# A first tile normalised after its projection, and a last tile in pieces of 384 and 128 columns

## The chip, the cores and the metric

The kernel runs on one core of one Trainium2 chip, as one program on five engines: TensorE (PE in the profile; its weight loads have a row of their own, PEld), VectorE (DVE), ScalarE (ACT), GpSimd (POOL) and SyncE (SP), which issues most of the transfers. The metric is the device time of one execution in microseconds (us), the lower the better.

## The reference, cut to what matters

Two request groups, 256 and 512 tokens of 1024 values each, go through the same two layers. Each layer has a token mixer (windowed attention in the first, differential attention in the second) and a dense channel mixer. Each of these four sub-layers stands between two norms:

```python
def rms_norm(x, g):
    y = x * lax.rsqrt(jnp.mean(x * x, axis=-1, keepdims=True) + RMS_EPS)
    return y * g

def swiglu(h, w_gate_up, w_down):
    g, u = jnp.split(h @ w_gate_up, 2, axis=-1)
    return (jax.nn.silu(g) * u) @ w_down

for i in range(DEPTH):                                   # DEPTH = 2
    h = rms_norm(x, norm_mix_pre[i])
    m = window_gqa_sink(h, ...) if i % 2 == 0 else diff_attention(h, ...)
    x = x + rms_norm(m, norm_mix_post[i])
    h = rms_norm(x, norm_ffn_pre[i])
    x = x + rms_norm(swiglu(h, ffn_w_gate_up[i], ffn_w_down[i]), norm_ffn_post[i])
```

The first thing that the first mixer does is one product, `qkv = h @ w_in`. A row of `x` divided by its root mean square is the row times one number, so that number may be applied before this product or after it.

## The kernel before, in words

The 768 tokens are six tiles of 128 rows, numbered 0 to 5. Every float32 product is made of three products of a rounded type (called fp32r in the rows): an operand is cut into a high part (`hi`, a cast on ACT) and the rest (`lo`, a subtraction on DVE), and hi by hi, hi by lo and lo by hi are added up in PSUM. These are lines 315, 316 and 317, with a new 128 by 128 weight load before each. The weights stream from DRAM and are cut the same way (lines 222 and 223).

At the start, `load_x`, `gain` and `fetch` queue on SP the loads of tile 0's x, of the first norm's gains (broadcast over the partitions into `gpre`), of two weight pieces, of tile 1's x and of two more weight pieces. For a tile, `enter` makes the normed rows: line 365 squares x and sums on ACT, line 359 adds epsilon on ACT, line 360 takes the power -1/2 on POOL, line 369 multiplies x by this number and by the gains on DVE. `entered` (and, for tile 0, the code below it) transposes the rows on PE (line 407), cuts them into hi and lo (lines 303 and 304), and enters the tile after the next. Two copies of an identity matrix in other types (lines 85 and 87) are made on DVE as well; the first transposes do not use them.

In `mixer_a`, `unit(i)` is the product of one tile with one of four groups of 384 columns (64 columns times four query heads, one key head and one value head). Its `end` reads the product from PSUM: the values (line 589, ACT) and the rotary positions (lines 530 to 536, DVE).

At the end, `ffn(1)` has seven products per tile over the columns of `w_down` (a product of 2 by 2 blocks in seven multiplications). In the last of them, tiles 3 and 4 each get 512 columns in one bank, and tile 5 gets its 512 columns in two pieces of 256 with a bank each (`last_product`), so that the first piece can be finished on DVE and ACT while PE makes the second. For each piece `k`, DVE adds what was there before (line 1169), ACT squares and sums (line 1291), and DVE multiplies by the gains (line 1293), in place. Then ACT and POOL make the norm's number (lines 359 and 360), and `last_tile` multiplies by it, adds x and stores, in two halves (lines 495 and 497). `begin(t)` loads the x that is added; its place is one of two buffers, and tile 5's buffer is the one from which tile 3's result is stored.

The order of the instructions on each engine is fixed when the program is built: a scheduler places them by priority and by its own estimate of when each is ready. Each engine then runs its own list strictly in that order and waits on semaphores.

Of the kernel before, what the change touches and what calls it, by code (L numbers as in the profile page):

```python
# [9 lines left out]
F32 = mybir.dt.float32  # L10
F32R = mybir.dt.float32r
BF16 = mybir.dt.bfloat16
AF = mybir.ActivationFunctionType
ALU = mybir.AluOpType
# [3 lines left out]
P = 128  # L18
D = 1024
KT = D // P  # L20
HD = 64
# [11 lines left out]
HALF = 384  # L33
# [13 lines left out]
def trunk(  # L47
# [19 lines left out]
    nc = tc.nc  # L67
    const = ctx.enter_context(tc.tile_pool(name="const", bufs=1))
# [3 lines left out]
    gpool = ctx.enter_context(tc.tile_pool(name="gpool", bufs=1))  # L72
# [5 lines left out]
    def bank(name):  # L78
        return ps.tile([P, 512], F32, tag="ps", name=name)
# [26 lines left out]
    nsink = const.tile([P, 16], F32, name="nsink")  # L106
    subl = const.tile([P, 1], F32, name="subl")
    nlam = const.tile([P, 1], F32, name="nlam")

    def small_inputs():  # L110
        nc.sync.dma_start(out=cos_sb, in_=cos)
# [79 lines left out]
    def load(dst, src):  # L191

        with ExitStack() as after:
            if dpool[0] is not None:
                after.enter_context(tc.issue_after(state["load"].ins))
            state["load"] = nc.sync.dma_start(out=dst, in_=src)
# [166 lines left out]
    def row_rstd(src, junk, name):  # L363
        ss = small.tile([P, 1], F32, tag="ss", name=f"ss_{name}")
        nc.scalar.activation(out=junk, in_=src, func=AF.Square, scale=D ** -0.5, accum_out=ss)
        return rstd(ss, eps_sb[:, 0:1], name)

    def scaled(y, src, r, g):
        state["scaled"] = nc.vector.scalar_tensor_tensor(out=y, in0=src, scalar=r, in1=g, op0=ALU.mult, op1=ALU.mult)

    def new_y(name):
        return scr.tile([P, D], F32, tag="y", name=f"y_{name}")
# [16 lines left out]
    x_at = [x_in]  # L389
# [134 lines left out]
    def rope(ap, dst, src, n, t, name):  # L524

        pos = t - seq_of(t)[0]
        t1 = ap.tile([P, n, HD], F32, tag="rope1", name=f"r1_{name}", bufs=1)
        t2 = ap.tile([P, n, HD], F32, tag="rope2", name=f"r2_{name}", bufs=1)
        h = HD // 2
        nc.vector.tensor_tensor(  # L530
            out=t1[:, :n], in0=src, in1=cos_sb[:, pos:pos + 1, :].broadcast_to([P, n, HD]), op=ALU.mult)
        nc.vector.tensor_tensor(
            out=t2[:, :n, :h], in0=src[:, :, h:], in1=sin_sb[:, pos:pos + 1, :h].broadcast_to([P, n, h]), op=ALU.mult)
        nc.vector.tensor_tensor(
            out=t2[:, :n, h:], in0=src[:, :, :h], in1=sin_sb[:, pos:pos + 1, h:].broadcast_to([P, n, h]), op=ALU.mult)
        nc.vector.tensor_tensor(out=dst, in0=t1[:, :n], in1=t2[:, :n], op=ALU.add)
# [30 lines left out]
    def mixer_a(gp, g_next, first_steps, o):  # L567
        with ExitStack() as st:
# [4 lines left out]
            def unit(i):  # L573

                gi, t = divmod(i, NT)
                first, n = seq_of(t)
                if t == 0:
                    wk[gi] = column_blocks(take(4), HALF)
                elif t in (2, 4):
                    free(6 - t // 2)  # L580
                pm = bank(f"pqa_{i}")
                steps = product_steps(pm[:, :HALF], [(htile(t, k), wk[gi][k]) for k in range(KT)])
                if t == NT - 1:
                    steps = releasing(steps, 4, 2)

                def end():
                    if t == first:
                        vv[gi, first] = ap.tile([P, n, HD], F32, tag=f"v{first}", name=f"va{gi}_{first}", bufs=2)
                    nc.scalar.copy(out=vv[gi, first][:, t - first], in_=pm[:, 320:384])
                    qk = ap.tile([P, 5, HD], F32, tag="qk", name=f"qk{i}", bufs=2)  # L590
                    rope(ap, qk, pm[:, :320].rearrange("p (n d) -> p n d", d=HD), 5, t, f"a{i}")

                    sp = ap.tile([P, 6, 2, HD], F32R, tag="sp", name=f"sp{i}", bufs=2)
                    nc.scalar.copy(out=sp[:, 0:4, 0], in_=qk[:, 0:4])
                    nc.scalar.copy(out=sp[:, 4], in_=qk[:, 4:5].broadcast_to([P, 2, HD]))
                    nc.vector.tensor_tensor(
                        out=sp[:, 0:4, 1], in0=qk[:, 0:4], in1=sp.bitcast(F32)[:, 0:4, 0], op=ALU.subtract)
                    nc.vector.tensor_tensor(
                        out=sp[:, 5], in0=qk[:, 4:5].broadcast_to([P, 2, HD]), in1=sp.bitcast(F32)[:, 4], op=ALU.subtract)

                    def turn():
                        if t == first:
                            kh[gi, first] = ap.tile([P, n * P], F32R, tag=f"kh{first}", name=f"kha{gi}_{first}")
                            kl[gi, first] = ap.tile([P, n * P], F32R, tag=f"kl{first}", name=f"kla{gi}_{first}")
                        q[i] = ap.tile([P, 4, P], F32R, tag="q", name=f"qa{i}", bufs=4)
                        tq, tk = ps.tile([P, 512], F32R, tag="ps", name=f"tqa{i}"), ps.tile([P, 512], F32R, tag="ps", name=f"tka{i}")
                        at = slice((t - first) * P, (t - first + 1) * P)
                        for j in range(2):
                            nc.tensor.transpose(tk[:, j * P:(j + 1) * P], sp[:, 4 + j].rearrange("p a d -> p (a d)"), ident_r)
                        for j in range(4):  # L610
                            nc.tensor.transpose(tq[:, j * P:(j + 1) * P], sp[:, j].rearrange("p a d -> p (a d)"), ident_r)
                        nc.scalar.copy(out=kh[gi, first][:, at], in_=tk.bitcast(F32)[:, 0:P])
                        nc.scalar.copy(out=kl[gi, first][:, at], in_=tk.bitcast(F32)[:, P:2 * P])
                        nc.scalar.copy(out=q[i].rearrange("p h n -> p (h n)"), in_=tq.bitcast(F32))

                    pending[i] = turn

                return steps + [end]
# [321 lines left out]
    def ffn(layer, later, comb, cpool, cstack, ostack, gains):  # L940
# [182 lines left out]
        with ExitStack() as st:  # L1123
# [7 lines left out]
            def run(p, gs, wk, tiles, into, first=None, last=None, w=512, part=0, more=True):  # L1131

                gs = list(gs)
                todo = [(g, j) for g in gs for j in range(min(2, NPAIR - 2 * g))]
                for n, (g, j) in enumerate(todo):
                    a = acts.of(p, g)
                    b = tuple(v[:, j * 512 + part:j * 512 + part + w] for v in wk[g])
                    for i in tiles:
                        products(
                            into[i][:, :w], [(tuple(v[:, j, i * P:(i + 1) * P] for v in a), b)],  # L1140
                            first and n == 0, bool(last) and n == len(todo) - 1, more and p > 2)
# [16 lines left out]
            def begin(t):  # L1158
                x_of[t] = xpool.tile([P, D], F32, tag="x", name=f"x{sub}_{t}")
                load(x_of[t], x_at[sub][t])  # L1160
# [7 lines left out]
            def add(t, c, b):  # L1168
                nc.vector.tensor_tensor(out=y[t][:, c], in0=b, in1=y[t][:, c], op=ALU.add)
# [56 lines left out]
            free(2)  # L1226

            V2 = [bank(f"pv2_{k}") for k in range(2)] if final else []

            def last_product(i, gs, wk, first=False, last=False, parts=(0, 1)):  # L1230

                if final and i == 2:
                    for k in parts:
                        run(6, gs, wk, [i], {i: V2[k]}, first, last, 256, 256 * k, False)
                else:
                    run(6, gs, wk, [i], V, False, last)

# [14 lines left out]
            free(0)  # L1252
            stage(2, 3)
            begin(4)
            gs = range(3, NGRP)
            wk = dict(zip(gs, take(3)))
            for g in gs:
# [26 lines left out]
            for k in range(2):  # L1284
                last_product(2, gs, wk, last=True, parts=(k,))
                if k == 0:
                    stage(4, 1)
                    begin(5)
                c = slice(256 * k, 256 * k + 256)
                add(5, c, V2[k][:, :256])  # L1290
                nc.scalar.activation(
                    out=junk[:, c], in_=y[5][:, c], func=AF.Square, scale=D ** -0.5, accum_out=ss4[:, k:k + 1])
                nc.vector.tensor_tensor(out=y[5][:, c], in0=y[5][:, c], in1=gp[:, c], op=ALU.mult)
                if k == 0:
                    nc.scalar.activation(out=ss[:, 0:1], in_=ss4[:, 0:1], func=AF.Identity, bias=ss[:, 0:1])
# [67 lines left out]
    y_in = {}  # L1363

    def enter(t):
        x = xs_sb[t]
        y_in[t] = new_y(f"pre0_{t}")
        scaled(y_in[t], x, row_rstd(x, y_in[t], f"pre0_{t}"), g_in)

    def entered(t):  # L1370
# [108 lines left out]
```

## Time and profile before

| what | value |
|---|---|
| time, median of 3 runs | 1687.2 us (1686.35 to 1689.65) |
| the profiled execution's own time | 1688.34 us |
| its span, first to last instruction | 1686.6 us |
| PE busy | 1659.1 us, 98% of the span |
| DVE, ACT, POOL busy | 1251.3, 949.7 and 81.7 us (74%, 56%, 5%) |
| mean granted TensorE clock | 0.997 |

PE is busy nearly everywhere, so the table says that a microsecond can be gained only where PE waits or where PE has nothing left to do. Rows of the timeline tell where that is: a row starts with its start and its duration in us, and a bracket at its end gives how long the engine had been idle before it and what ended the wait. A matmul's row is longer than the time between two of them, since they are pipelined; the time between the starts of neighbours is its pace.

### The profile page before, as it was taken

Reading aid. Unit: us, or ns where it says so; the run is one execution under the profiler, and the core shown is the slowest. Engines: PE = TensorE matmul, PEld = TensorE weight load, DVE = VectorE, ACT = ScalarE, POOL = GpSimd, SP = SyncE. Lnnn points to the kernel's source line nnn. Section 1 sums busy time; section 2 is a strip of 40 time slices with the busy share of each in tenths; the row PEclk is TensorE's granted clock in tenths of the full one; section 3 lists DMA queues with packets and bytes.
Section 4 is the critical chain, followed back from the end, with each engine's and each line's share of the span. In section 5 each row is a group of like instructions: output and inputs, shape, how many; then the busy total and the mean of one; then the engine's idle time right before and its main releaser. Section 6 shows DMA issues by size and latency. Waiting matters only on the chain. (4 is left out here: it accounts for less than half of the span.)

```text
span 1686.6 us, 25513 instructions
## 1 busy us (share of the span) xinstructions
PE 1659.1 (98%) x9483; PEld 1514.3 (90%) x9483; DVE 1251.3 (74%) x2488; ACT 949.7 (56%) x2158; POOL 81.7 (5%) x104
## 2 busy tenths in 40 slices
PE   7999999999999999999999999999899999999998
PEld 7888878899999998888999999988799999998887
DVE  7888766896766666988777676874997666666886
ACT  6777775654444444556566666674744444444553
POOL 1000001000000000001000000331000000000001
PEclk9999999999999999999999999999999999999999
DMA  6111014534333347666211111113444343336765
GB/s 212 39 38 48 14 38 150 175 134 140 109 125 99 128 139 250 230 235 205 83 39 38 38 38 38 48 51 113 170 138 141 108 141 108 128 114 226 249 222 176
DMA packets 62107, 207.30 MB, mean 123 GB/s; under 512 B 6752, under 2 KB 8928, under 8 KB 61728
## 3 DMA queue, kind: packets, MB, share of 16 engines
q1 hardware_dynamic: 55152, 175.15, 30.8%
q0 software_dynamic: 6688, 30.28, 5.6%
q8 instruction: 74, 1.21, 0.3%
q14 instruction: 49, 0.40, 0.1%
q10 hardware_dynamic: 144, 0.26, 0.0%
HBM read 162.80 MB, written 42.86 MB: 122 GB/s over the span
## 5 line engine op out<-in xcount | busy, mean ns | idle before, releaser
L223 DVE TENSOR_TENSOR wlo<-wraw,whi 128x1024 fp32r<-128x1024 f32 (+2 forms) x180 | 204.9, 1144 | 173.9 <-ACT whi L222 172.7
L222 ACT CAST whi<-wraw 128x1024 fp32r<-128x1024 f32 (+2 forms) x180 | 176.5, 986 | 117.4 <-PE py L316 58.9
L315 PE MATMUL py<-hhi,whi 128*128 128x384 f32 x464 | 155.4, 335 | 0.8 <-ACT u L976 0.8
L317 PE MATMUL py<-hhi,wlo 128*128 128x384 f32 x464 | 155.0, 334 | 0.0
L316 PE MATMUL py<-hlo,whi 128*128 128x384 f32 x464 | 155.0, 334 | 0.0
L315 PE MATMUL pqb<-whi,hhi 128*128 128x384 f32 x384 | 136.5, 356 | 0.0
L316 PE MATMUL pqb<-wlo,hhi 128*128 128x384 f32 x384 | 128.9, 336 | 0.0
L317 PE MATMUL pqb<-whi,hlo 128*128 128x384 f32 x384 | 128.8, 335 | 0.0
L303 ACT CAST hhi<-araw 128x768 fp32r<-128x768 f32 (+1 forms) x74 | 57.6, 783 | 94.6 <-DMA araw<-act 94.2
L317 PE MATMUL pv<-whi,hlo 128*128 128x512 f32 (+1 forms) x240 | 92.2, 384 | 0.4 <-DVE hlo L304 0.4
L315 PE MATMUL pv<-whi,hhi 128*128 128x512 f32 (+1 forms) x240 | 92.4, 385 | 0.0
L316 PE MATMUL pv<-wlo,hhi 128*128 128x512 f32 (+1 forms) x240 | 92.1, 384 | 0.0
L304 DVE TENSOR_TENSOR hlo<-araw,hhi 128x768 fp32r<-128x768 f32 (+1 forms) x74 | 65.2, 889 | 32.3 <-ACT hhi L303 32.1
L315 PEld LDWEIGHTS py<-hhi,whi 128*128 128x128 f32 x464 | 87.1, 188 | 1.7 <-ACT u L976 1.4
L316 PEld LDWEIGHTS py<-hlo,whi 128*128 128x128 f32 x464 | 87.1, 188 | 0.0
L317 PEld LDWEIGHTS py<-hhi,wlo 128*128 128x128 f32 x464 | 87.1, 188 | 0.0
L315 PE MATMUL po<-whi,hhi 128*128 128x512 f32 x192 | 77.9, 406 | 0.2 <-ACT hhi L303 0.2
L317 PE MATMUL po<-whi,hlo 128*128 128x512 f32 x192 | 75.4, 393 | 0.2 <-DVE hlo L304 0.2
L316 PE MATMUL po<-wlo,hhi 128*128 128x512 f32 x192 | 75.3, 392 | 0.0
L315 PEld LDWEIGHTS pqb<-whi,hhi 128*128 128x128 f32 x384 | 72.3, 188 | 2.0 <-issue 1.7
L315 PE MATMUL pqa<-whi,hhi 128*128 128x384 f32 x192 | 73.9, 385 | 0.0
L315 PE MATMUL px<-hhi,whi 128*128 128x384 f32 x208 | 70.8, 342 | 2.7 <-ACT hhi L303 2.7
(303 smaller groups left out, 4829.6 us busy)
## 6 DMA issues: line engine op xcount, KB each, us to landing
act<-st POOLq DMA_DIRECT2D x22, 1344.0 KB, 6.6
wraw<-in_wgu SPq DMA_DIRECT2D x56, 512.0 KB, 4.6
araw<-act SPq DMA_DIRECT2D x70, 384.0 KB, 4.0
y_wraw<-in_wgu SPq DMA_DIRECT2D x40, 512.0 KB, 3.6
wraw<-in_wd SPq DMA_DIRECT2D x40, 512.0 KB, 3.9
wraw<-in_wb SPq DMA_DIRECT2D x32, 384.0 KB, 3.2
xd<-x SPq DMA_DIRECT2D x18, 512.0 KB, 3.0
x<-xd SPq DMA_DIRECT2D x18, 512.0 KB, 4.1
```

Of the source, the lines that this page charges most:

```text
L222: state["raw_hi"] = nc.scalar.copy(out=hi, in_=src)
L223: state["raw_lo"] = nc.vector.tensor_tensor(out=lo, in0=src, in1=hi.bitcast(F32), op=ALU.subtract)
L303: state["hi"] = nc.scalar.copy(out=hi, in_=src)
L304: state["lo"] = nc.vector.tensor_tensor(out=lo, in0=src, in1=hi.bitcast(F32), op=ALU.subtract)
L315: nc.tensor.matmul(out, ah, bh, start=start and i == 0, stop=False, skip_group_check=more)
L316: nc.tensor.matmul(out, ah, bl, start=False, stop=False, skip_group_check=more)
L317: nc.tensor.matmul(out, al, bh, start=False, stop=stop and i == last, skip_group_check=more)
```

## The change

There are three parts, and one of the places is in two functions.

First, tile 0's rows are no longer multiplied by the norm's number before they are transposed: `enter(0)` multiplies x by the gains alone, and the number goes into a small tile `r0` (a copy on POOL). The squares go to a scratch buffer of their own. In `mixer_a`, the four products of tile 0 are read from PSUM once, by an ACT instruction that multiplies by `r0` and writes a tile `pm0` in SBUF; the values and the rotary positions then read this tile.

Second, in the last `ffn`, tile 5's x is loaded right behind tile 4's, into the place of `gpre`, which the last sub-layer doesn't use.

Third, tile 5's two pieces have 384 and 128 columns in place of 256 and 256.

```diff
 def end():
+    src = pm
+    if t == 0:
+        src = ap.tile([P, HALF], F32, tag="pm0", name=f"pm0_{gi}")
+        nc.scalar.activation(out=src, in_=pm[:, :HALF], func=AF.Copy, scale=r0)
     if t == first:
         vv[gi, first] = ap.tile([P, n, HD], F32, tag=f"v{first}", name=f"va{gi}_{first}", bufs=2)
-    nc.scalar.copy(out=vv[gi, first][:, t - first], in_=pm[:, 320:384])
+    nc.scalar.copy(out=vv[gi, first][:, t - first], in_=src[:, 320:384])
     qk = ap.tile([P, 5, HD], F32, tag="qk", name=f"qk{i}", bufs=2)
-    rope(ap, qk, pm[:, :320].rearrange("p (n d) -> p n d", d=HD), 5, t, f"a{i}")
+    rope(ap, qk, src[:, :320].rearrange("p (n d) -> p n d", d=HD), 5, t, f"a{i}")
...
 V2 = [bank(f"pv2_{k}") for k in range(2)] if final else []
+cols = [slice(0, 384), slice(384, 512)]
...
-            run(6, gs, wk, [i], {i: V2[k]}, first, last, 256, 256 * k, False)
+            run(6, gs, wk, [i], {i: V2[k]}, first, last, cols[k].stop - cols[k].start, cols[k].start, False)
...
 begin(4)
+if final:
+    x_of[5] = gpool.tile([P, D], F32, tag="gpre", name=f"x{sub}_5")
+    load(x_of[5], x_at[sub][5])
...
     if k == 0:
         stage(4, 1)
-        begin(5)
-    c = slice(256 * k, 256 * k + 256)
-    add(5, c, V2[k][:, :256])
+    c = cols[k]
+    add(5, c, V2[k][:, :c.stop - c.start])
...
 def enter(t):
     x = xs_sb[t]
     y_in[t] = new_y(f"pre0_{t}")
+    if t == 0:
+        state["scaled"] = nc.vector.tensor_tensor(out=y_in[t], in0=x, in1=g_in, op=ALU.mult)
+        nc.gpsimd.tensor_copy(out=r0, in_=row_rstd(x, new_y("sq0"), "pre0_0"))
+        return
     scaled(y_in[t], x, row_rstd(x, y_in[t], f"pre0_{t}"), g_in)
```

The scheduler also moves instructions. On DVE at the start of the program, these are the rows before (`y_pre` is the tile's rows before the transposes, `tp_h` the transposed rows in PSUM, `wlo` and `hlo` the lo parts of weights and rows, `ident_r` and `ident_b` the two copies of the identity):

```order
L85 CAST ident_r<-ident 128x128
L87 CAST ident_b<-ident 128x128
L369 SCALAR_TENSOR_TENSOR y_pre_0_162<-x_0_138,rstd_pre_0_165,gpre_140 128x1024
L223 TENSOR_TENSOR wlo_170<-wraw_142,whi_169 128x768
L223 TENSOR_TENSOR wlo_176<-wraw_144,whi_175 128x768
L304 TENSOR_TENSOR hlo_113<-tp_h_0_0_181,hhi_111 128x4x128
L304 TENSOR_TENSOR hlo_113<-tp_h_0_1_188,hhi_111 128x4x128
```

and now:

```order
L1378 TENSOR_TENSOR y_pre_0_163<-x_0_139,gpre_141 128x1024
L224 TENSOR_TENSOR wlo_173<-wraw_143,whi_172 128x768
L85 CAST ident_r<-ident 128x128
L87 CAST ident_b<-ident 128x128
L224 TENSOR_TENSOR wlo_179<-wraw_145,whi_178 128x768
L305 TENSOR_TENSOR hlo_114<-tp_h_0_0_184,hhi_112 128x4x128
L305 TENSOR_TENSOR hlo_114<-tp_h_0_1_191,hhi_112 128x4x128
```

The first multiplication has lost an operand, and the two casts of the identity stand between the two `wlo`. The list of ACT is the same there: the two weight casts stand ahead of tile 0's `hhi`.

On DVE at the end of the program (`yf` is the sub-layer's result, `pv` a bank, `x` the tile that is added and stored), before:

```order
L1154 TENSOR_TENSOR yf_4_16415<-pv_1_16600,gpost_16144 128x512
L472 SCALAR_TENSOR_TENSOR x_4_17567<-yf_4_16415,rstd_post_4_17610,x_4_17567 128x1024
L1169 TENSOR_TENSOR yf_5_16416<-pv_0_17474,yf_5_16416 128x256
L1169 TENSOR_TENSOR yf_5_16416<-pv_1_17475,yf_5_16416 128x256
L1293 TENSOR_TENSOR yf_5_16416<-yf_5_16416,gpost_16144 128x256 x2
L495 SCALAR_TENSOR_TENSOR x_5_17632<-yf_5_16416,rstd_last,x_5_17632 128x512 x2
```

and now:

```order
L1159 TENSOR_TENSOR yf_4_16426<-pv_1_16611,gpost_16155 128x512
L473 SCALAR_TENSOR_TENSOR x_4_17578<-yf_4_16426,rstd_post_4_17623,x_4_17578 128x1024
L1174 TENSOR_TENSOR yf_5_16427<-pv_0_17485,yf_5_16427 128x384
L1301 TENSOR_TENSOR yf_5_16427<-yf_5_16427,gpost_16155 128x384
L1174 TENSOR_TENSOR yf_5_16427<-pv_1_17486,yf_5_16427 128x128
L1301 TENSOR_TENSOR yf_5_16427<-yf_5_16427,gpost_16155 128x128
L496 SCALAR_TENSOR_TENSOR x_5_17580<-yf_5_16427,rstd_last,x_5_17580 128x512 x2
```

The first piece's multiplication by the gains, which writes in place and waits until ACT has squared the piece, now stands ahead of the second piece's addition. On SP, tile 5's load moves from behind tile 3's store to ahead of it; nothing else moves there at the end.

## Rows read from the trace of the kernel before

**Rows 1.** Waits of PE, whole span: in total, times, longest (us)

```profile
PE tp_h L407 <- DVE y_pre L369: 8.1, 1, 8.1
```

**Rows 2.** Tile `gpre`, 0 to 20 us: issue (duration ns, start) and landing

```profile
L376 SPq DMA_DIRECT2D gpre<-in_g_pre x1: 421/421/421, 1.2 to 1.2; - x1
...
DMA to landing us min/median/max: 5.4/5.4/5.4
```

**Rows 3.** Timeline of all engines, first 12 us

```profile
1.45 0.45 DVE L85 CAST ident_r<-ident 128x128 fp32r<-128x128 f32 x1 [0.52 <-POOL ident masks.py:199]
...
1.67 0.30 DVE L87 CAST ident_b<-ident 128x128 bf16<-128x128 f32 x1
...
5.82 0.55 POOL L360 TENSOR_TENSOR rstd_pre<-rstd_pre,mhalf 128x1 f32<-128x1 f32 x1 [4.00 <-ACT rstd_pre L359]
...
6.76 1.28 DVE L369 SCALAR_TENSOR_TENSOR y_pre<-x,rstd_pre,gpre 128x1024 f32<-128x1024 f32 x1 [4.79 <-POOL mask_r L93]
...
8.52 2.02 DVE L223 TENSOR_TENSOR wlo<-wraw,whi 128x768 fp32r<-128x768 f32 x2 [0.48 <-ACT whi L222]
8.71 0.83 ACT L222 CAST whi<-wraw 128x768 fp32r<-128x768 f32 x1 [0.23 <-DMA wraw<-in_wa]
...
9.45 1.24 ACT L303 CAST hhi<-tp_h 128x512 fp32r<-128x512 f32 x2
...
11.19 0.69 PE L317 MATMUL pqa<-whi,hlo 128*128 128x384 f32 x1
```

**Rows 4.** The same timeline, two later weight loads of PE

```profile
18.10 0.86 PEld L407 LDWEIGHTS tp_h<-ident,y_pre 128*128 128x128 f32 x8 [0.42 <-DVE y_pre L369]
...
23.58 0.19 PEld L317 LDWEIGHTS pqa<-whi,hlo 128*128 128x128 f32 x1 [0.51 <-DVE hlo L304]
```

**Rows 5.** Timeline of all engines, from 1675 us

```profile
1675.65 0.28 PE L315 MATMUL pv<-whi,ahi 128*128 128x256 f32 x1
...
1675.85 0.60 ACT L1153 ACTIVATE y_pd<-pv 128x512 f32<-128x512 f32 x1 [2.32 <-PE pv L317]
...
1676.57 0.69 DVE L1154 TENSOR_TENSOR yf<-pv,gpost 128x512 f32<-128x512 f32 x1 [1.10 <-ACT y_pd L1153]
...
1677.59 1.28 DVE L472 SCALAR_TENSOR_TENSOR x<-yf,rstd_post,x 128x1024 f32<-128x1024 f32 x1 [0.33 <-POOL rstd_post L360]
...
1678.79 0.42 DVE L1169 TENSOR_TENSOR yf<-pv,yf 128x256 f32<-128x256 f32 x1
...
1679.12 0.28 PE L317 MATMUL pv<-whi,alo 128*128 128x256 f32 x1
1679.24 0.42 ACT L1291 ACTIVATE y_last<-yf 128x256 f32<-128x256 f32 x1 [2.31 <-DVE yf L1169]
...
1679.98 0.40 ACT L1291 ACTIVATE y_last<-yf 128x256 f32<-128x256 f32 x1
...
1680.94 0.55 POOL L360 TENSOR_TENSOR rstd_last<-rstd_last,mhalf 128x1 f32<-128x1 f32 x1 [3.38 <-ACT rstd_last L359]
1682.15 1.42 DVE L495 SCALAR_TENSOR_TENSOR x<-yf,rstd_last,x 128x512 f32<-128x512 f32 x2 [1.21 <-DMA x<-xd]
```

**Rows 6.** Timeline of PE, 899 to 906 us, in the second mixer

```profile
899.97 0.33 PE L315 MATMUL pqb<-whi,hhi 128*128 128x384 f32 x1
...
901.88 0.34 PE L317 MATMUL pqb<-whi,hlo 128*128 128x384 f32 x1
...
902.27 1.06 PE L871 MATMUL pob<-vb,aT 128*128 128x128 f32 x8
903.09 0.42 PE L315 MATMUL pqb<-whi,hhi 128*128 128x384 f32 x1
```

**Rows 7.** Timeline of PE, 25.2 to 26.4 us: transposes of fp32r

```profile
25.93 0.51 PE L611 MATMUL tqa<-ident_r,sp 128*128 128x128 f32 x4
26.28 0.41 PE L315 MATMUL pqa<-whi,hhi 128*128 128x384 f32 x1
```

**Rows 8.** Groups of weight loads by form: busy us, mean ns, idle before

```profile
L315 PEld LDWEIGHTS pv<-whi,ahi 128*128 128x128 f32 x35 | 6.6, 189 | 1.0
```

More of the change, by code (lines that the diff above doesn't have):

```diff
@@ L108, in trunk @@
     nlam = const.tile([P, 1], F32, name="nlam")
+    r0 = const.tile([P, 1], F32, name="r0")
     def small_inputs():
```

## Prediction

> **What bounds the kernel now.** I read the page first: PE is busy 98% of the span, so a change can pay only where PE waits or after its last product. The view of waits says where PE waits: one wait of 8.1 us, at the start, for tile 0's normed rows [rows 1]; no other single wait comes near it. So there are two places, and the timeline is read there: the first 25 us, where the order in which DMA, ACT and DVE get ready decides, and the last 11 us, from tile 5's first piece at 1675.65 to the last multiplication at 1682.15 and the store behind it [rows 5]. In between, every product and every weight load stays as it is.
>
> **Start: the norm's number.** It leaves the path, but was it last? The power on POOL ends at 5.82 + 0.55 = 6.37. The gains, which the same DVE instruction reads, were issued at 1.2 and landed 5.4 later, at 6.6 [rows 2], and the instruction began at 6.76 [rows 3]. The bracket there names POOL because POOL's next instruction ended late; the transfer is the later one. The new multiplication needs the gains as well, so it begins at 6.7 or so and saves at most 0.1.
>
> Nor would an earlier end help. ACT casts the second weight piece from 8.71 to 9.54 (it waits for that transfer), and tile 0's `hhi` stands behind it and begins at 9.45 [rows 3]. ACT's list is the same now. The first product therefore starts when it did.
>
> **Start: the moved casts.** In DVE's new list the two identity casts stand behind the first `wlo`. Before, they ran from 1.45 to 1.97, 0.52 together, in idle time. The two `wlo` ran back to back from 8.52 to 10.54, and `hlo` followed; the first product that needs `hlo` started at 11.19 [rows 3]. Now the first `wlo` ends at 8.52 + 1.01 = 9.53, when the second piece's cast is just done (9.54), so the casts push the second `wlo` and both `hlo` by about 0.45 to 0.5, and the product at 11.19 goes to about 11.65. I take +0.45.
>
> Some of this comes back. Before, PE's weight loads waited twice more, 0.42 us for tile 2's rows and 0.51 us for tile 2's `hlo` [rows 4]. A load runs one product ahead, so each costs the products that less one pace of 0.17: 0.25 and 0.34. In the new lists tile 1's first `hlo` stands ahead of tile 2's multiplication, tile 2's transposes stand seven products later, and tile 2's first `hlo` stands ahead of tile 3's multiplication. Both waits should go: -0.59. Together with the 0.1 the start is worth 0.45 - 0.59 - 0.1, about -0.2. Bounds: -0.7 (the casts find a gap) to +0.5 (both waits stay).
>
> The four reads of tile 0's product cost ACT some 0.5 us each (a 384-column read, by the widths below), in a stage in which PE is the bound; POOL's copy is beside the path. I take 0.
>
> **End: tile 5's x.** Before, the last multiplication began at 1682.15, after a wait of 1.21 for x. The norm's number was there at 1680.94 + 0.55 = 1681.49 [rows 5]. With x loaded early, what is late next is that number: a gain of 1682.15 - 1681.52 = 0.63, if nothing else moves. The load itself goes out behind tile 4's, more than ten us ahead, and no queue waits for it.
>
> **End: the pieces.** Each of tile 5's eleven blocks takes three products per piece, so 33 pairs of products (18 before the last five blocks, 15 in them). A 256-column product has a pace of (1679.12 - 1675.65)/29 = 0.1197 [rows 5], a 384-column one of (901.88 - 899.97)/11 = 0.1736 [rows 6]. A pair was 0.2394 and is 0.1736 + c, where c is the pace of a 128-column fp32r product with its own weight load. The trace has none, so c is bounded:
> - The line through 384 and 256 gives 0.1197 - 0.0539 = 0.066, the lower end: the pair costs the same as before.
> - Four 128-column fp32r transposes, each with its own load, took 26.28 - 25.93 = 0.35, or 0.087 each [rows 7].
> - Eight records of the plain float32 product of 128 columns took 903.09 - 902.27 = 0.82 [rows 6]; the program has two records for each such product, so 0.205, the upper end.
>
> I take c = 0.12. The weight load does not get shorter with the columns (0.189 in this stage, for pieces of 512 and 256 columns [rows 8]), and a 256-column product is the narrowest fp32r product that the trace shows behind such a load.
>
> The Trainium skill (TensorE: Matmul & The Clock Gate, section "LDWEIGHTS (loading the stationary operand)") says that a load takes the number of columns over 1.2 ns, so 107 ns for 128, whatever the product's width. That rule speaks against this change: c could not fall under 0.107, and the sum by it would be +0.8 at the end in place of +1.1. The load's row of 0.189 is longer than the rule's figure, but rows overlap, so the row does not refute it.
>
> Now the chain. PE's 18 early pairs push all that follows by 18 x (0.1736 + 0.12 - 0.2394) = 0.97, tiles 3 and 4 too. Tile 4's multiplication goes from 1677.59 to 1678.56 and ends at 1679.84. Widths: DVE took 0.69 for 512 and 0.42 for 256 columns, so 0.56 for 384 and 0.29 for 128; ACT 0.60 and 0.42, so 0.51 and 0.30 [rows 5]. The first piece's addition runs 1679.76 to 1680.32, its square to 1680.86 and its sum is read by 1680.96; then DVE multiplies this piece in place until 1681.54, and only then adds the second piece, 1681.46 to 1681.75. (PE is done with it by 1681.1, so PE is not what it waits for.) Before, the second square started at 1679.98 and the number was ready at 1681.52, 1.54 later; the narrower square takes 0.10 less. So the second square starts at 1681.78 and the last multiplication at 1681.78 + 1.44 = 1683.22, against 1682.15: **+1.07**. With c at its lower end the same steps give 1682.24, +0.09: DVE's new order alone eats the 0.63. In between it is 0.09 + 18 x (c - 0.066).
>
> **Sum.** -0.2 + 1.07 = +0.87 on the span of 1686.6, so 1687.5; the profiled execution took 1.74 more than its span, so 1689.2 against its 1688.34. It lies 1.14 above the median of the runs shown; on the median, 1687.2 + 0.87 = 1688.05. I forecast 1688.0: no change that can be told.
>
> **Rivals.**
> - *The narrow products are cheap.* c between 0.066 and 0.087: +0.09 to +0.47 at the end, -0.2 at the start, so 1687.1 to 1687.5. For it: the transposes' pace. Against it: the transposes only move data, and their loads need not be those of a product. The Trainium skill (the same page, section "Back-to-back issue gap") gives about 81 ns for a load and a 128-column product; by it the end would be +0.36 and the time 1687.4; the transposes' 0.087 is near it, and no row shows it for a product.
> - *The narrow products cost as much as plain float32 ones* (the slower side). c = 0.205: the push is 18 x 0.139 = 2.51, the second piece's products run from 1680.76 to about 1684.0 and now PE is what the second addition waits for; square at 1684.36, multiplication at 1685.80, +3.65; with the start 1690.6. Place: PE, the 33 narrow products. It makes the kernel slower by more than 0.2% only from c of about 0.2. For it: the float32 rows. Against it: fp32r transposes of the same width take less than half.
> - *The start gains after all.* The bracket at 6.76 is right, POOL was the last and the gains were there when the power began. Then the multiplication moves up by 6.76 - 5.82 = 0.94, and all behind it, if ACT's list lets it: the start gives -0.94 in place of -0.2 and the time is 1687.2 + 1.07 - 0.94 = 1687.3; with cheap products as well, 1686.35. Against it: the gains' landing and the weight casts ahead of `hhi`.
>
> **How the numbers follow.** Chances: forecast 0.47, cheap products 0.25, dear products 0.18, start gains 0.10. The likeliest gives 1688.0. The range starts at 1686.35 less the runs' own spread (0.85 below their median), 1685.5, and reaches over the dear products with the start's upper bound, 1691.3. A measurement of this kernel tells about 0.2%, 3.4 us, from no change. Only the dear products come near that, and about half of them pass it: 0.09, and 0.06 for a wait in the reordered stage of the first mixer that I don't see: 0.15 slower. No case gains 3.4; 0.06 for what I don't see and the runs' spread. The rest, 0.79, is no change.
>
> **What would show it.** In the profile after: the first multiplication still begins near 6.7; the product that waits for the first `hlo` starts near 11.65; the waits of 0.42 and 0.51 are gone. At the end, the narrow products start 0.12 apart; the last multiplication begins near 1683.2 in a span that is otherwise the same, with no wait for x ahead of it; DVE's multiplication of the first piece ends just before the second addition. I am wrong if the first multiplication begins before 6, if the narrow products are 0.2 apart, or if the time moves by over 3.4.

## The result, and the profile after

The changed kernel took 1692.95 us (median of 6 runs, 1692.16 to 1694.67), the kernel before 1688.32 (6 runs, 1686.35 to 1690.51): ratio 1.0029, 95% interval [1.0016, 1.0042]. It is slower by some 4.6 us, and the forecast of 1688.0, with its range up to 1691.3, was wrong. The profiled execution took 1692.68 us, with a span of 1690.9 and a mean clock of 0.999.

**Where the time went.** PE's list of products is the same up to the tail, but for 38 that stand in another order (at 18 to 20, 55 to 57 and 169 to 171 us), so the start of the same product can be compared in the two traces. How much later it stands in the changed kernel, stretch by stretch (times of the kernel before):

| stretch, us | what is there | after less before, us |
|---|---|---|
| 0 to 24 | start | -0.40 |
| 24 to 297 | first mixer | +0.05 |
| 297 to 345 | first ffn begins | -1.81 |
| 345 to 626 | first ffn's products | **+1.44** |
| 626 to 756 | its down projection | +0.03 |
| 756 to 759 | PE waits for `y_pd` | +1.57 |
| 759 to 1240 | second mixer, second ffn begins | +0.89 |
| 1240 to 1512 | second ffn's products | **+1.43** |
| 1512 to 1660 | its down projection | +0.12 |
| 1660 to the last multiplication | tail | +1.02 |

The sum is 4.34; the spans differ by 4.3. The tail came out nearly as forecast (+1.02 against +1.07). The rest lies where I had said that nothing happens, and a part of it is chance, as is shown below: the -1.81 and the +1.57.

**The start.** PE's first wait, the view of waits of the changed kernel (answers [rows 1]; in total, times, longest, us):

```profile
PE tp_h L408 <- DVE y_pre L1378: 8.2, 1, 8.2
```

and the timeline of all engines up to 11.3 us (answers [rows 3]):

```profile
5.85 0.55 POOL L361 TENSOR_TENSOR rstd_pre<-rstd_pre,mhalf 128x1 f32<-128x1 f32 x1 [4.03 <-ACT rstd_pre L360]
...
6.79 1.23 DVE L1378 TENSOR_TENSOR y_pre<-x,gpre 128x1024 f32<-128x1024 f32 x1 [5.86 <-DMA gpre<-in_g_pre]
...
9.40 0.22 DVE L85 CAST ident_r<-ident 128x128 fp32r<-128x128 f32 x1
...
9.53 0.22 DVE L87 CAST ident_b<-ident 128x128 bf16<-128x128 f32 x1
9.67 0.95 DVE L224 TENSOR_TENSOR wlo<-wraw,whi 128x768 fp32r<-128x768 f32 x1
...
10.54 1.28 DVE L305 TENSOR_TENSOR hlo<-tp_h,hhi 128x512 fp32r<-128x512 f32 x2
...
11.27 0.69 PE L318 MATMUL pqa<-whi,hlo 128*128 128x384 f32 x1 [0.23 <-DVE hlo L305]
```

With the norm out of the way the bracket at 6.79 names the gains' DMA: the norm was not the last input. The two casts start 0.13 us apart and push the second `wlo` by 0.14, not by 0.45, so the product that needs `hlo` starts at 11.27, against 11.19. The forecast for that product was 11.65. The two later waits of [rows 4] are gone: no such row stands in PEld's timeline from 17 to 25 us.

**The tail** (the timeline of all engines from 1679 us; answers [rows 5]):

```profile
1679.88 0.33 PE L316 MATMUL pv<-whi,ahi 128*128 128x384 f32 x1
...
1681.81 1.29 DVE L473 SCALAR_TENSOR_TENSOR x<-yf,rstd_post,x 128x1024 f32<-128x1024 f32 x1 [0.32 <-POOL rstd_post L361]
1683.01 0.55 DVE L1174 TENSOR_TENSOR yf<-pv,yf 128x384 f32<-128x384 f32 x1
...
1683.60 0.52 ACT L1299 ACTIVATE y_last<-yf 128x384 f32<-128x384 f32 x1 [2.45 <-DVE yf L1174]
...
1683.90 0.27 PE L317 MATMUL pv<-wlo,ahi 128*128 128x128 f32 x1
1684.01 0.28 PE L318 MATMUL pv<-whi,alo 128*128 128x128 f32 x1
...
1684.25 0.56 DVE L1301 TENSOR_TENSOR yf<-yf,gpost 128x384 f32<-128x384 f32 x1 [0.68 <-ACT y_last L1299]
1684.72 0.28 DVE L1174 TENSOR_TENSOR yf<-pv,yf 128x128 f32<-128x128 f32 x1
1685.04 0.31 ACT L1299 ACTIVATE y_last<-yf 128x128 f32<-128x128 f32 x1 [0.50 <-DVE yf L1174]
...
1685.91 0.55 POOL L361 TENSOR_TENSOR rstd_last<-rstd_last,mhalf 128x1 f32<-128x1 f32 x1 [4.13 <-ACT rstd_last L360]
1686.49 1.42 DVE L496 SCALAR_TENSOR_TENSOR x<-yf,rstd_last,x 128x512 f32<-128x512 f32 x2 [0.72 <-POOL rstd_last L361]
```

The 128-column products are 0.11 apart (forecast 0.12); PE is done at 1684.01, and the second addition stands at 1684.72 behind DVE's multiplication of the first piece, as forecast.

**The middle.** Products of the first ffn, the PE timeline of the kernel before (start, duration of the modelled record):

```profile
409.47 0.33 PE L315 MATMUL py<-hhi,whi 128*128 128x384 f32 x1
409.65 0.33 PE L316 MATMUL py<-hlo,whi 128*128 128x384 f32 x1
409.82 0.33 PE L317 MATMUL py<-hhi,wlo 128*128 128x384 f32 x1
409.99 0.33 PE L315 MATMUL py<-hhi,whi 128*128 128x384 f32 x1
410.17 0.33 PE L316 MATMUL py<-hlo,whi 128*128 128x384 f32 x1
```

and the same five products after:

```profile
407.56 0.35 PE L316 MATMUL py<-hhi,whi 128*128 128x384 f32 x1
407.75 0.34 PE L317 MATMUL py<-hlo,whi 128*128 128x384 f32 x1
407.92 0.34 PE L318 MATMUL py<-hhi,wlo 128*128 128x384 f32 x1
408.10 0.33 PE L316 MATMUL py<-hhi,whi 128*128 128x384 f32 x1
408.28 0.33 PE L317 MATMUL py<-hlo,whi 128*128 128x384 f32 x1
```

Before, their starts span 0.70, after 0.72. I call the time from one such start to the next a gap. From 350 to 620 us nearly all gaps between 384-column products are 173 or 174 ns before (12 of 1556 are 175 or more); after, 374 of 1547 are 175 or more. Both profiles have three gaps of 250 to 290 ns within the first 15 us of this stretch; apart from them the longest is 185. No wait is recorded there and the granted clock is 1.00. The view of windows counts the products; columns: stretch, sum, PE busy (products), granted clock, DMA share, GB/s. Before:

```profile
350.00:620.00 270.00, 270.00 (x1557) 1.00 0.38 125
```

After:

```profile
350.00:620.00 270.00, 270.00 (x1549) 1.00 0.37 126
```

Eight products fewer in the same time, at 0.1735 each 1.4 us. PE shows as busy all the time in both: the share of busy time hides it.

### The profile page after: what moved, and what is told of

The parts are those of the page before. It is cut to its first block, busy times and chain, and to the rows that moved or that the text cites. A ratio compares the mean times of both kernels' runs of the same rounds, so it can differ in the third digit from the quotient of the medians.

```text
span 1690.9 us, 25510 instructions
## 1 busy us (share of the span) xinstructions
PE 1661.0 (98%) x9483; PEld 1516.7 (90%) x9483; DVE 1251.6 (74%) x2488; ACT 951.0 (56%) x2162; POOL 82.9 (5%) x105
## 5 line engine op out<-in xcount | busy, mean ns | idle before, releaser
L318 PE MATMUL pv<-whi,hlo 128*128 128x512 f32 (+2 forms) x240 | 92.5, 385 | 0.4 <-DVE hlo L305 0.4
L316 PE MATMUL pv<-whi,hhi 128*128 128x512 f32 (+2 forms) x240 | 92.6, 386 | 0.3 <-DVE yf L1174 0.3
L317 PE MATMUL pv<-wlo,hhi 128*128 128x512 f32 (+2 forms) x240 | 92.4, 385 | 0.0
L317 PEld LDWEIGHTS pqb<-wlo,hhi 128*128 128x128 f32 x384 | 72.4, 188 | 0.6 <-DVE wlo L224 0.5
```

What stands on the lines that cost most here:

```text
L316: nc.tensor.matmul(out, ah, bh, start=start and i == 0, stop=False, skip_group_check=more)
L317: nc.tensor.matmul(out, ah, bl, start=False, stop=False, skip_group_check=more)
L318: nc.tensor.matmul(out, al, bh, start=False, stop=stop and i == last, skip_group_check=more)
```

## The experiments

**Theories.** The ffn's instructions are the same, but the new tile `r0` holds 4 bytes per partition and takes a slot of 32, ahead of nearly all tiles of the left side of SBUF. So weights, `hhi`, `hlo` and the rest lie 32 bytes higher, and nearer to the tiles of the right side. Two kinds of these matter here: `s1`, `s2` and `s4` (each in a hi and a lo part), combined blocks of the ffn's input that are stationary operands of its products just as `hhi` and `hlo` are, and the ffn's kept parts, into which ScalarE copies results. A stationary operand is the 128 by 128 block that a weight load brings; the weights of the model are what streams past it. *Address theory*: the new addresses slow the products. It has two forms. In *theory K*, which I took up first, ScalarE's copies into the kept parts collide with what TensorE reads; in *theory S*, TensorE's own operands collide. *Rival*: the loss comes from the start, the tail and the chance course of DMAs and clock.

**Padding alone, and the change without it.** e1_pad32 and e2_pad64 are the kernel before with a wider constant tile; e3 and e4 are the whole change.

```diff
-nlam = const.tile([P, 1], F32, name="nlam")
+nlam = const.tile([P, 16], F32, name="nlam")[:, 0:1]   # e1; 24 columns in e2
...
-r0 = const.tile([P, 1], F32, name="r0")                # e3, in the changed kernel
+r0 = eps_sb[:, 2:3]                                    # eps_sb has 3 columns
...
+edge = ctx.enter_context(tc.tile_pool(name="edge", bufs=1, side="right"))   # e4, in the changed kernel
+nc.gpsimd.memset(edge.tile([P, 8], F32, name="edge"), 0.0)
```

> The kernel before with one constant tile made 32 bytes wider per partition (nlam, 64 bytes in place of 32); no instruction is added, removed or moved, but every tile allocated behind it on the left side of SBUF, the weights, h and u among them, lies 32 bytes higher, as it does in the changed kernel. Address theory (the miss comes from the 32 bytes that the new tile r0 takes, which make ScalarE's writes into tiles of the right side and TensorE's reads from tiles of the left side collide): 1.8 to 4 us slower, ratio 1.0011 to 1.0024, and between 350 and 620 us the 384-column products start 174.5 ns apart on average, with some of 176 to 185, in place of 173.5. Rival (the miss comes from the start, the tail and the chance course of DMAs): ratio 1.0000 within 0.0005, and 173.5 ns with nothing above 175.

> The kernel before with the same constant tile made 64 bytes wider (96 in place of 32), so that all that lies behind it is 64 bytes higher. Address theory, if the position within 64 bytes is what counts: ratio 1.0000 within 0.0005, all ffn products 173.5 ns apart. Address theory, if any move against the right side counts: 1.0011 to 1.0024 and 174.5 ns, as with 32 bytes. Rival without addresses: 1.0000 as well, so this run tells only together with the one of 32 bytes.

> The changed kernel, whole, with r0 as a third column of the tile eps_sb (8 of its 32 bytes are used), so that no address moves. Address theory: most of the loss goes; what is left is the tail's +0.9 less the start's -0.4, so 0.3 to 1.2 us slower than before, ratio 1.0002 to 1.0007, and ffn products 173.5 ns apart. Rival (start, tail and chance): still 1.0020 to 1.0032.

> The changed kernel, whole, with r0 as it is, and a 32-byte tile put first into the right side of SBUF, so that the tiles of the right side (the ffn's kept parts, the combined activations, the mixers' pools) move by 32 bytes as well and lie to the left side as they did before. Address theory by the distance between what is read and what is written: ratio 1.0002 to 1.0007, products 173.5 ns apart. Address theory by the place of TensorE's own operands: still 1.0020 to 1.0032 and 174.5 ns. Rival without addresses: 1.0020 to 1.0032, but products as before's in the undisturbed stretches.

Measured: e1 1.0014 [1.0005, 1.0022], e2 1.0008 [0.9999, 1.0017], e3 1.0015 [1.0004, 1.0025], e4 1.0006 [0.9997, 1.0014]. The kernel before itself ran from 1684.91 to 1693.61 beside them, so the times put e1 and e3 above 1, leave e2 and e4 open, and can't tell the theories apart (e1's interval, 0.8 to 3.7 us, holds 2.9). The products can. Mean gap from 350 to 620 us: before 173.56 ns, after 174.47, e1 174.43, e2 173.70, e3 173.54, e4 173.68. e1, in which no instruction differs from before, has the whole slowing (345 to 626 us +1.40, 1240 to 1512 us +1.43). Its window:

```profile
350.00:620.00 270.00, 270.00 (x1550) 1.00 0.36 124
```

e3, the whole change with `r0` in spare bytes, has none of it:

```profile
350.00:620.00 270.00, 270.00 (x1557) 1.00 0.38 125
```

In e4 the left side is 32 bytes up and the right side 32 down, in e2 the left is 64 up: both come 64 nearer, and both show the same small rest (31 and 32 gaps of 176, 24 of 182). The rival falls for these 2.9 us. So does my expectation that in e4 the two sides lie to each other as before: the right side grows downwards, so e4 doubled the shift. e3's ratio stands above its expected 1.0002 to 1.0007, of which only the upper part lies in its interval. (In e3, as in the changed kernel, the squares' own scratch buffer makes some scratch tiles exchange two buffers of 4096 bytes; the pace doesn't show it.)

**The changed kernel again, and its parts without the 32 bytes.** e5 is the changed kernel; e6 to e8 are the kernel before with one part each (e8 with `r0` in `eps_sb`).

```diff
+    x_of[5] = gpool.tile([P, D], F32, tag="gpre", name=f"x{sub}_5")   # e6, and begin(5) goes
+    load(x_of[5], x_at[sub][5])
...
+cols = [slice(0, 384), slice(384, 512)]                              # e7
...
+    state["scaled"] = nc.vector.tensor_tensor(out=y_in[t], in0=x, in1=g_in, op=ALU.mult)   # e8, with pm0 and src
```

> The changed kernel once more, unaltered, beside the parts below. Address theory (2.9 us of the loss are the ffn's products, 1.4 in each ffn, and come with every run): ratio 1.0020 to 1.0030, products between 350 and 620 us 174.5 ns apart, the stretches 345 to 626 us and 1240 to 1512 us each 1.3 to 1.5 us longer than before's. If the wait of TensorE for y_pd at 758 us (1.4 us in the first profile) belongs to the slower ffn, it is there again; if it was chance, it is under 0.4 us. Rival (chance course of the runs): ratio under 1.0015.

> The kernel before with x of the last tile loaded into the gains' place at the start of the last groups, and nothing else of the change. All theories: the last multiplication no longer waits for x, so from the first piece of tile 5's last blocks to that multiplication it takes 5.8 to 6.0 us in place of 6.50; 0.5 to 0.7 us faster, ratio 0.9996 to 0.9997, which the scatter of the runs may hide; products of the ffn 173.5 ns apart.

> The kernel before with the last pieces of 384 and 128 columns, and x loaded where it was. Step of the prediction: the 18 pairs of products take 18 times 0.05 us longer, so the last blocks begin 0.9 us later; the shorter last piece gives back at most 0.3 before the last multiplication, which then still waits for x. 0.6 to 1.0 us slower, ratio 1.0004 to 1.0006. Rival (the narrow pieces also slow the tail itself): more than 1.2 us slower.

> The kernel before with the first tile's norm applied to its projections, r0 as a third column of eps_sb (no address of a weight or of h moves), and before's tail. Prediction's step: the transposes still start when the gains have landed and been multiplied, 8.1 to 8.2 us; 0 to 0.4 us gained by 24 us, ratio 0.9997 to 1.0001. Rival (the norm left the path, so its 2 us and more are gained): transposes at 7 us or before, ratio 0.9990 or less. Rival (the copies of the projections on ScalarE cost later): ratio above 1.0005.

Measured: e5 1.0018 [1.0008, 1.0028], e6 0.9996 [0.9986, 1.0005], e7 1.0006 [0.9996, 1.0016], e8 0.9998 [0.9989, 1.0007].
- e5 repeats the gaps (174.47) and the two stretches (+1.44, +1.41). Its ratio is a little under the expected 1.0020 to 1.0030. Its PE never waits for `y_pd`, while e14 below, with no slowed products, waits 2.2 us there; so the 1.57 us at 758 belong to one execution, not to the change.
- e6: the last product starts at 1681.14 and the last multiplication at 1683.54, 2.40 later; before it was 3.03, so the 0.63 is there:

```profile
1682.95 0.55 POOL L360 TENSOR_TENSOR rstd_last<-rstd_last,mhalf 128x1 f32<-128x1 f32 x1 [3.38 <-ACT rstd_last L359]
1683.54 1.41 DVE L495 SCALAR_TENSOR_TENSOR x<-yf,rstd_last,x 128x512 f32<-128x512 f32 x2 [0.59 <-POOL rstd_last L360]
```

- e7: the 18 early pairs push by 0.90 (from 1660 to the product at 1675.65), and from the last product at 1681.28 to the multiplication at 1683.77 it is 2.49, with no wait for x although x is loaded where it was:

```profile
1683.77 1.42 DVE L495 SCALAR_TENSOR_TENSOR x<-yf,rstd_last,x 128x512 f32<-128x512 f32 x2 [0.73 <-POOL rstd_last L360]
```

  So with 384 and 128 columns the early x gains nothing (2.48 in the changed kernel), and without them it gains 0.63.
- e8: the start stands at -0.94 at 24 us. The five other runs with this start part have -0.68 to +0.23, the nine other runs without it -0.89 to +1.15: at most some tenths.

**Which tiles, which period.** All four are the kernel before with padding, one profile each. Here and in e13 the expectations say "larger" of a distance where the sides come nearer by that amount; and e10's 160 and e9's 128 are sums of the two moves.

```diff
 comb = {...}                                              # s1, s2, s4
+gpool2.tile([P, 24], F32, name=f"pad{layer}")             # e9, on e1; 8 columns in e10
...
 ga[c] = temp("ga", c, AHEAD + 1, cpool)
+if c == 0:
+    cpool.tile([P, 24], F32, name=f"top{layer}")          # e10, on e1
...
+nlam = const.tile([P, 32], F32, name="nlam")[:, 0:1]      # e11; 40 columns in e12
```

> The kernel with one constant tile 32 bytes wider (as in e1_pad32), and a 96-byte gap put behind the combined activations s1, s2 and s4 in their pool, so that these six tiles move down by 96 bytes: their distance to h and to the weights is then 128 bytes larger than before, while the ffn's kept parts (sv, ku, kv, kw, ga) stay 32 bytes nearer. For the pace of the 384-column products alone, 350 to 620 us. Theory S (TensorE's own operands collide where it goes from stationary tiles of the left side, h, to those of the right, s, or back; period 128 bytes or less): 173.5 to 173.7 ns, all of them undisturbed. Theory K (ScalarE's copies into the kept parts collide with TensorE's reads): 174.2 ns or more, slow products during the copies kw<-pw.

> The kernel with one constant tile 32 bytes wider (as in e1_pad32), and gaps of 32 bytes behind s1, s2 and s4 and of 96 bytes behind the kept parts, so that the kept parts move down by 96 bytes (distance to the left side 128 bytes larger than before) and s1, s2, s4 by 128 (distance 160 larger, which in steps of 128 is 32). Theory S: 174.4 ns between 350 and 620 us, as with the 32 bytes alone. Theory K: 173.5 to 173.8 ns.

> The kernel before with the constant tile nlam 96 bytes wider, so that all behind it on the left side lies 96 bytes higher. Either theory, if the distance between the sides counts and 32 bytes gave 174.4 and 64 bytes 173.7 ns: 96 bytes is the mirror image of 32 in a period of 128, so 174.0 to 174.5 ns if the collision is symmetric; 173.5 if it is not.

> The kernel before with the constant tile nlam 128 bytes wider. If the collision repeats every 128 bytes: 173.5 ns between 350 and 620 us, none above 175, as in the kernel before. If it depends on the plain distance or on a longer period: above 173.6.

| left side and `s1`, `s2`, `s4` nearer by | runs | products in 350 to 620 us | mean gap, ns | gaps of 175 or more |
|---|---|---|---|---|
| 0 bytes | before, e3, e6, e7, e8 | 1557 to 1558 | 173.52 to 173.56 | 6 to 12 |
| 32 | after, e5, e1, e13 (below) | 1549 to 1550 | 174.43 to 174.47 | 369 to 398 |
| 64 | e2, e4 | 1556, 1557 | 173.70, 173.68 | 83, 78 |
| 96 | e11 | 1545 | 175.02 | 497 |
| 128 | e12, e9 | 1546, 1547 | 174.75, 174.75 | 487, 491 |
| 160 | e10 | 1541 | 175.45 | 745 |

The period of 128 that I had supposed is wrong (for e12 it gave 173.5). So the numbers expected of e9, e10 and e11, which rested on it, missed too: e9's 174.75 even lies where theory K was to put it, e10's 175.45 and e11's 175.02 above all that I had named. But e9 and e12 reach 128 by different moves, the kept parts coming 32 nearer in e9 and 128 in e12, and agree almost to the gap: 70 and 71 of 181 ns. So theory K falls, and theory S stands in the form "the distance between the left side and `s1`, `s2`, `s4`". The windows view of e10:

```profile
350.00:620.00 270.00, 270.00 (x1541) 1.00 0.36 123
```

**The six tiles alone.** e13 is the kernel before with one line more:

```diff
 comb = {...}
+gpool2.tile([P, 8], F32, name=f"pad{layer}")
```

> The kernel before with a gap of 32 bytes behind s1, s2 and s4 in their pool and nothing else, so that these six tiles lie 32 bytes lower and no weight, no h and no kept part moves; their distance to the left side is 32 bytes larger. If the distance between TensorE's own operands is enough: 174.45 ns on average between 350 and 620 us, with 36 or so products at 185 ns, the same pattern as in e1_pad32, and 345 to 626 us takes 1.4 us longer. If other tiles (weights against h, the kept parts, u, the raw weights) are needed for it: 173.5 to 173.7 ns.

Measured: 174.44 ns, 37 gaps of 185, and 345 to 626 us +1.43. Its window:

```profile
350.00:620.00 270.00, 270.00 (x1550) 1.00 0.37 123
```

Nothing but the stationary tiles `s1`, `s2` and `s4` (hi and lo, the six of each layer) moved, by 32 bytes. That settles what causes the 2.9 us: where these tiles lie against the left side. (Its 1698.91 us are one execution with a wait of 2.2 for `y_pd` and with half the clock granted at 303, 763 and 1200 us; the time of a single run says nothing here.)

**The parts that are worth keeping.** e14 is e6 and e8 together.

> The first tile's norm applied to its projections with r0 as a third column of eps_sb, x of the last tile loaded early, last pieces of 256 and 256 columns as before. From the parts: the start gives 0 to 0.4 us, x 0.6, nothing is pushed and no address of an operand of the ffn moves: 0.5 to 1.1 us faster than before, ratio 0.9993 to 0.9998, and from the last product to the last multiplication 2.4 us in place of 3.03. Against it stands only the scatter of the runs.

Measured: 0.9993 [0.9984, 1.0003]; gaps of 173.54 ns; last product 1683.02, last multiplication 1685.41, 2.39 later. It is as expected, but the scatter of the runs does not let one call it faster than the kernel before.

## Why the prediction was wrong

- **The step that failed** is the last sentence of its first part: "In between, every product and every weight load stays as it is." The list of instructions does, but for the order of a few; their operands' addresses do not. I read the diff's line `r0 = const.tile([P, 1])` as a tile without cost and none of the rivals was about SBUF. It costs +1.44 and +1.43 us, 2.9 of the loss. In all: 2.9, the tail's 1.0 and a start near 0 make 3.9 or so, between the two measured ratios (1.0029 and 1.0018, 4.9 and 3.0 us).
- **What the step does not explain.** The forecast missed by 4.95 us, and 1688.0 with the 2.9 added would still lie in its range. Another 1.1 is the base: the three runs of the kernel before that I added to had a median of 1687.2, the six beside the changed kernel have 1688.32. The 1.0 or so that is left is within the scatter of the runs, and no experiment assigns it.
- The Trainium skill (SBUF — State Buffer, section "Operand start alignment") asks of an operand's start that it be a multiple of the element's size, and says of itself that this is about legality, not speed. The moves of the table are multiples of 32 bytes, so all of them keep that rule for these 4-byte elements, and the products' pace differs by up to 1.1% between them: an address that is allowed can still be a slow one.
- **Start, the norm's number**: right. The gains' DMA is now named as the last input and the first multiplication began at 6.79 (forecast 6.7). **The moved casts**: mis-sized, 0.14 in place of 0.45; two casts whose records last 0.22 start 0.13 apart. **The later waits**: right, both gone. The sum, -0.2 in bounds of -0.7 to +0.5, stands against -0.40 and, over the runs, nearly nothing: the start without the change varies more than that at 24 us.
- **Tail**: right. c, the pace of a narrow product, was taken as 0.12 and is 12 gaps from 1682.67 to 1684.01, 0.112 each; the push of 0.97 was 0.90; DVE's new order held the second addition back; +1.07 was +1.02. The cheap rival (up to 0.087) and the dear one (0.205) both fall. The Trainium skill's rule (TensorE: Matmul & The Clock Gate, section "LDWEIGHTS (loading the stationary operand)") gives 107 ns for a load of 128 columns. The measured 0.112 agrees with it within 5 ns, but the 0.087 of the transposes, each with its own load [rows 7], lies under it, and no run here shows that the load is what sets the 0.112. e6 and e7 show one thing that I could have seen: the early x and the narrow last piece shorten the same stretch, from the last product to the last multiplication (3.03 before, 2.40 and 2.49 with one of them, 2.48 with both), so only one of them can be had.
- **What was chance.** Beside that, the compared profiles differ by -2.37 us from 297 to 308 us and by +1.57 at 758. The windows view of the kernel before:

```profile
303.00:308.00 5.00, 5.00 (x16) 0.50 0.90 285
```

and after:

```profile
303.00:308.00 5.00, 5.00 (x30) 1.00 0.80 278
```

The first profile ran these five microseconds at half clock (1.2 GHz, 16 products), the second at the full one (2.4 GHz, 30 products), behind waits for the same operands of the first ffn. e2, with other addresses and no other instruction, has 0.59 there and e13 0.50; e6 has 0.64 from 1236 to 1240 us, at the start of the second ffn. Other profiles have such a stretch elsewhere, e3 and e4 near 1193 and 1220 us. So one profile against another can be 2 us off at such a place whatever the change, and a base profile has to be read with that in mind.

## What to carry to other kernels

A new tile, however small, moves the tiles that are allocated behind it, and in this kernel products that wait for nothing ran 0.5 to 1.1% slower for such a move alone. Look at the gaps between starts of like products in a steady stretch: here they had one value where undisturbed, and a spread without waits pointed to addresses. A pad that moves no instruction, as in e1, tells it at once. Put a number that must be kept into spare bytes of a tile that exists, as e3 did.

## What the runs showed of the hardware that I had not expected

In these runs the pace of 384-column fp32r products depends on where the stationary tiles `s1`, `s2` and `s4` lie against the left side: 173.5 ns at the distance of the kernel before, 174.45 with 32 bytes less, 175.45 with 160 less, not monotonic (173.7 at 64). With 32 bytes the slow ones, 175 to 185 ns, are the first products after PE goes from `h` to `s1`, `s2`, `s4` or back; with 128 they come through the whole of the `s` products, one gap of 181 or 182 in every five, so each 0.88 us:

```profile
403.10 0.34 PE L316 MATMUL py<-s2lo,whi 128*128 128x384 f32 x1
403.28 0.34 PE L317 MATMUL py<-s2hi,wlo 128*128 128x384 f32 x1
```

(PE timeline of e9: 103 to 284, 181 ns.) That two accesses of TensorE collide is inferred from the distances, not seen in a row. Which two, whether weight load and streamed operand or two loads, and whether the pattern repeats at a longer distance, stays open: no run here tells it. That another engine's copies are not needed follows from the pairs that agree whatever the kept parts did (e9 and e12, e1 and e13), not from a run without copies.
